# A streaming encoder trunk on one core: other chunks in one FFN, its last down products onto doubled x in PSUM, and eight weight sums made by an accumulating transfer

## The chip, the core and the metric

The kernel runs on one core of one Trainium2 chip. A core has a matrix engine (TensorE, in the profile PE, with its weight loads PEld), a vector engine (VectorE, DVE), an activation engine (ScalarE, ACT), GpSimd (POOL) and a queue that issues transfers (SyncE, SP); POOL and ACT issue some transfers too. SBUF is the core's working memory. PSUM is the memory into which PE's products go and in which they add up; here it holds eight banks of 128 x 512 f32, and DVE and ACT read it. The metric is the device time of one execution in microseconds (us); the time before is 2503.59 us, the median of 3 runs (2502.64 to 2503.89).

## The reference, cut to what matters

Two groups of streams (512 new frames, and 8 x 16 sample frames, together T = 640 columns) go through two layers; all is float32.

```
for l in range(2):
    x = x + 0.5 * swiglu1(rmsnorm(x))        # FFN "a{l}"
    x = x + mixer(rmsnorm(x))                # short convolution and chunk-band attention, gated
    x = x + 0.5 * swiglu2(rmsnorm(x))        # FFN "b{l}"
y = rmsnorm(x)

swiglu(h) = (silu(h @ w_g) * (h @ w_u)) @ w_down      # 1024 -> 2816 -> 1024
```

The outputs are y, the new keys and values, and the convolution's new state rows.

## The kernel before, in words

**Layout.** x is kept in SBUF as KT = 8 tiles of 128 x 640 (features by tokens); a product of one 128 x 128 weight block takes the tokens in two halves of HT = 320 columns. A float32 operand is split into a high part (hi, rounded by an ACT copy) and a low part (lo, what is left, by a DVE subtraction), and each product is three matmuls: hi by hi, lo by hi, hi by lo.

**The weight stream.** All weights are laid out on the host as one stream of 128 x 1024 rows (wst), in the order in which they are used. load (L253) lets SP fetch a row into a raw buffer; four buffers turn, so a row is fetched when DVE has read the one whose place it takes. prep (L308) makes the hi part (whi, ACT, L321) of the next slab, flush (L324) its lo part (wlo, DVE, L326); slab and begin call prep two slabs ahead of use. Both engines keep their own order: an instruction that waits holds up those behind it.

**Seven products for eight.** Where it can, the kernel multiplies 2 x 2 blocks with seven products instead of eight (block, L405, matmul L411; for the down weights down_rows, L966, matmul L982). For that the weights of a unit of two stream rows ra and rb are combined by source (L271) into four slabs: slab 0 is ra; slab 1 is a sum s = rb's two halves and ra's first (two adds); slab 2 is ra's first half plus rb's first half (L299, one DVE add of 128 x 512), and s plus ra's second half (L300); slab 3 is rb's second half. In such a unit gate_up (L773) makes one unit of 128 hidden features, gate and up together, in the order X11, X21, XN6, XT5, XT7, X22, XT4; after X11, XN6 and XT5 an ACT copy (c1, u2, c5: L850, L863, L866) takes a partial result from PSUM, and a later product adds to or overwrites that bank only after the copy. Hidden units that go into a down product by seven are made in pairs: Pair.product (L911) multiplies gate and up, and rounds the operand with an ACT copy (L926) and a DVE subtraction (L931); it runs in the tail of a unit, that is while the next unit is multiplied.

**Chunks.** The 22 hidden units of an FFN are taken in chunks (FFNS, L46). While the units of a chunk are made, the down products of the chunk before are put between them. A chunk of 4 that isn't the last goes down by seven products (by_seven, L81), in two calls of down_rows of 84 matmuls, which send part of their results to x by accumulating transfers of POOL (L1004) and add the rest with DVE (L1009). Any other chunk goes down by plain products (steps and product, L391 to L403, matmul L388): one per output tile m, with 6 matmuls for each hidden unit of the chunk, and then DVE's x[m] = x[m] + 0.5 * PSUM (L1119). The last chunk's are plain and come last, tile by tile, and the next stage's operands are made from each x[m] as soon as it is there (Expand.final, L539: square and gain on ACT, differences on DVE, hi parts on ACT, lo parts on DVE; Expand.weights, L594, prepares the next weights in the last tiles). PSUM has two accumulators of two banks for such products (acc) and four banks for the rest (att).

**Order.** PE's order is written out. DVE's and ACT's too (ORDERED, L213) at the beginning and the end of an FFN; between the third unit of its first by-seven chunk and the "cut" before its last products a scheduler orders them. POOL and SP are ordered by the scheduler.

**Where the diff touches.** FFNS (L46), source, prep and flush, multiply, steps and product (L384 to L403), Expand.weights (L594), gate_up (L773), Pair.product (L911), ffn (L1049). The FFNs named a0, b0, a1, b1 follow each other with a mixer between a and b of a layer. Line numbers in this section and in the profile before are those of the kernel before.

Of the kernel before, what the change touches and what calls it, by code (L numbers as in the profile page):

```python
# [44 lines left out]

FFNS = {"a0": ((4, 4, 4, 4, 4, 2), 4), "b0": ((2, 4, 4, 4, 8), 0),  # L46
        "a1": ((4, 4, 4, 4, 4, 2), 0), "b1": ((3, 4, 4, 4, 4, 3), 0)}
# [10 lines left out]

MARGIN = 2, 4

XT4, XN6, XT7, X21, X22, X11, XT5 = range(7)
# [128 lines left out]
def trunk(ctx: ExitStack, tc: tile.TileContext, xin, wst, small, pbias, samplebias, kcache, vcache,  # L190
# [59 lines left out]
    raws, ready = [], []  # L250
    sums, pool, spool = {}, [None], [None]

    def load(i):  # L253
# [17 lines left out]
    def source(i):  # L271
# [3 lines left out]
        if i not in sources:  # L275
# [6 lines left out]
            else:  # L282
# [14 lines left out]
                elif arg == 2:  # L297
                    if kind == "gu":
                        add(ra[:, h1], ra[:, h1], rb[:, h1])  # L299
                    add(ra[:, h2], sums.pop(n)[:, h1], ra[:, h2])  # L300
                    sources[i] = [(ra, whole)]
                else:
                    sources[i] = [(rb, h2)]
        return sources[i]

    pending = []

    def prep(i):  # L308
# [9 lines left out]
        for src, c in parts:  # L318
            d = slice(o, o + c.stop - c.start)
            o = d.stop  # L320
            ACT.copy(hi[:, d], src[:, c])  # L321
            pending.append((lo[:, d], src[:, c], hi[:, d]))

    def flush():  # L324
        for lo, src, hi in pending:
            DVE.tensor_tensor(out=lo, in0=src, in1=hi.bitcast(F32), op=ALU.subtract)  # L326
        pending.clear()

    used = [0]
# [53 lines left out]

    def multiply(ps, ws, xs, first, last):  # L384
        (wh, wl), (xh, xl) = ws, xs
        for j, (w, x) in enumerate(((wh, xh), (wh, xl), (wl, xh))):
            for a in range(2):
                PE.matmul(ps[:, a, :HT], w, x[:, a * HT : (a + 1) * HT],  # L388
                          start=first and j == 0, stop=last and j == 2)

    def steps(ps, ops, at=()):  # L391


        n = len(ops)
        for k, (xh, xl) in enumerate(ops):
            if k in at:
                at[k]()
            multiply(ps, tiles.take(), (xh, xl), k == 0, k == n - 1)
            yield

    def product(ps, ops, at=()):
        for _ in steps(ps, ops, at):
            pass  # L403
# [122 lines left out]
    class Expand(Stats):  # L526
# [67 lines left out]
        def weights(self, m):  # L594


            if m == KT - 3:
                source(used[0] + 3)
            elif m == KT - 1:
# [130 lines left out]
    def seven(n, bank, X, c1, u2, c5, first, second, third, last):  # L730
# [39 lines left out]
        with soon():  # L770
            last(pa)

    def gate_up(fp, n, ex, first, tails, put, j, pair, later, at):  # L773

# [72 lines left out]
        else:  # L847
# [14 lines left out]
            mul(pa, s1, 0, XN6, every, False, True)  # L862
            ACT.copy(u2, pa)  # L863
            spot("e3")
            mul(pc, s1, 1, XT5, every, True, True)
# [18 lines left out]
        def tail(weights=True):  # L884
# [5 lines left out]
            if pair:  # L890
                pair.product(n, u, g, hi, lo)
            else:
# [9 lines left out]
    class Pair:  # L902
# [7 lines left out]

        def product(self, n, u, g, hi, lo):  # L911
            if self.E is None:
# [12 lines left out]
            flush()  # L925
            ACT.copy(halves(hi), z[:, at])  # L926
            self.low(halves(lo), halves(hi), z[:, at])
            self.keep(kinds, hi, lo)

        def low(self, lo, hi, z):  # L930
# [118 lines left out]
    def ffn(name, fp, ex, goff, after, end=False):  # L1049
# [7 lines left out]
        hold[0] = True  # L1057

        mode = ExitStack()
        free = min(j for j in range(FT) if by_seven(name, j)) + 2  # L1060
# [8 lines left out]
        for what, a in ffn_order(name):  # L1069
# [6 lines left out]
            if what == "gu":  # L1076
                pair = None
                if by_seven(name, a):
                    i, odd = divmod(a - chunk_at(name, a)[0], 2)
                    if not odd:  # L1080
                        at = chunk_at(name, a)[0]
                        rows = at and by_seven(name, at - 1)
                        pairs[a] = Pair(fp, f"{name}_{a}", i, later, TURNS[i if rows else i + 2])
                    pair = pairs[a - odd]
                gate_up(fp, f"{name}_{a}", ex, a == plain, tails, act.__setitem__, a, pair, later,
                        a - chunk_at(name, a)[0])
# [12 lines left out]
            if end and js[0] == last:  # L1099
                nxt.all([act[j] for j in js])  # L1100
                break
            for m, js in a:
                if js[0] == last and m < 2 and first_two:
# [851 lines left out]
```

## Time and profile before

| what | value |
|---|---|
| three runs | 2502.64, 2503.59, 2503.89 us |
| the profiled execution | 2503.67 us |
| its span, first to last instruction | 2501.9 us |
| granted TensorE clock | 0.999 of full |
| HBM read, written | 222.70 MB, 7.94 MB |
| stretch of b0 | about 837 to 1255 us |
| stretch of a1 | about 1255 to 1667 us |

A row of the profile that describes a group of instructions has the line of the kernel, the engine, the operation, output <- inputs by the program's names (numbers left out, so paa is pa of an a FFN, pab of a b FFN, and lent or raw any of that name), the shape, the count, then the busy time, the mean duration of one in ns, and the idle time before them with what ended it. A row of the waits has who waited on whom: us in all, times, longest. In the timeline a row begins with the start and the duration. A row of the stretches has the stretch, its length, and for PE, PEld, DVE, ACT and POOL the busy time with the number of instructions, then the clock, the share of the transfer engines and GB/s. A row of the transfers has the issuing queue, the count, the size and the time from issue to landing. Matmuls overlap in the rows, so the distance between starts, not the duration, is what one costs. Windows of a row begin with the span at 0.

### The profile page before, as it was taken

To read this page: it belongs to the slowest core of one execution; us is meant where nothing else is said; L and a number is where in the kernel's file an instruction comes from. 1 tells how busy PE (TensorE), PEld (TensorE's weight loads), DVE (VectorE), ACT (ScalarE), POOL (GpSimd) and SP (SyncE) were. 2 spreads that over 40 slices of the span, in tenths; PEclk is the share of its full clock that TensorE was granted. 3 is DMA by queue.
4 is the path that set the end of the run, shared out by engine and by line. 5 is a ranking of instruction groups with operands and counts; after the bars stand their busy time and mean duration, and the time that the engine had idled before them with its cause. 6 is when DMAs were issued, how large, how long until landed. Compare 5 with 4: busy or idle time off the path is not lost.

```text
span 2501.9 us, 43874 instructions
## 1 busy us (share of the span) xinstructions
PE 2483.4 (99%) x17472; PEld 2433.1 (97%) x17472; DVE 2125.5 (85%) x3455; ACT 1321.4 (53%) x2065; POOL 240.0 (10%) x378
## 2 busy tenths in 40 slices
PE   9999999999999999999999999999999999999998
PEld 8999999889999999999999999998999999999998
DVE  7889998888777899998699999988887768899997
ACT  7445556665444545555455555566644455455553
POOL 0001112111000001100001111121110000011111
PEclk9999999999999999999999999999999999999999
DMA  4233445335222234443224343443342222244433
GB/s 146 76 102 102 123 117 127 108 109 169 77 91 92 72 100 116 111 106 101 85 77 109 110 122 101 116 119 117 121 156 85 77 93 79 87 112 110 121 101 103
DMA packets 101005, 265.47 MB, mean 106 GB/s; under 512 B 11360, under 2 KB 46816, under 8 KB 100800
## 3 DMA queue, kind: packets, MB, share of 16 engines
q1 hardware_dynamic: 69408, 220.76, 27.2%
q0 software_dynamic: 30528, 41.26, 8.9%
q8 instruction: 137, 2.24, 0.4%
q10 hardware_dynamic: 864, 0.65, 0.1%
q14 instruction: 68, 0.56, 0.1%
HBM read 222.70 MB, written 7.94 MB: 92 GB/s over the span
## 4 chain that ended last, share of the span: by engine, by line
PE 95%; DVE 2%; ACT 1%; issue 1%; DMA 1%; SPq 0%; DVEq 0%; ACTq 0%; POOLq 0%
PE pab L411 12%; PE paa L411 11%; PE pcb L411 6%; PE pca L411 6%; PE daa L982 5%; PE py L388 4%; PE po L388 4%; PE qa L411 4%; PE dab L982 4%; PE pdb L388 4%; PE pbb L411 3%; PE pba L411 3%; PE dca L982 3%; PE ma_cv L411 2%; PE pda L388 2%; PE pv L1425 2%
## 5 line engine op out<-in xcount | busy, mean ns | idle before, releaser
L321 ACT CAST whi<-raw 128x1024 fp32r<-128x1024 f32 (+1 forms) x566 | 509.6, 904 | 404.4 <-DVE raw L265 48.6
L326 DVE TENSOR_TENSOR wlo<-raw,whi 128x1024 fp32r<-128x1024 f32 (+1 forms) x566 | 585.8, 1038 | 147.2 <-ACT whi L321 142.2
L321 ACT CAST whi<-s 128x1024 fp32r<-128x1024 f32 (+1 forms) x152 | 144.3, 950 | 267.3 <-issue 89.5
L411 PE MATMUL pab<-xhib,whi 128*128 128x320 f32 x704 | 218.0, 310 | 0.0
L411 PE MATMUL pab<-xlob,whi 128*128 128x320 f32 x704 | 217.4, 309 | 0.0
L411 PE MATMUL pab<-xhib,wlo 128*128 128x320 f32 x704 | 217.4, 309 | 0.0
L411 PE MATMUL paa<-xhia,whi 128*128 128x320 f32 x640 | 198.1, 310 | 0.8 <-ACT c_a L863 0.5
L411 PE MATMUL paa<-xloa,whi 128*128 128x320 f32 x640 | 197.6, 309 | 0.0
L411 PE MATMUL paa<-xhia,wlo 128*128 128x320 f32 x640 | 197.6, 309 | 0.0
L326 DVE TENSOR_TENSOR wlo<-s,whi 128x1024 fp32r<-128x1024 f32 (+1 forms) x152 | 166.3, 1094 | 2.8 <-ACT whi L321 2.8
L1004 POOL DMA_DIRECT2D x<-c_b x56 | 49.2, 1016 | 1070.0 <-DVE x L1009 786.4
L1004 POOL DMA_DIRECT2D x<-c_a x72 | 63.4, 1013 | 832.2 <-ACT whi L321 508.7
L411 PEld LDWEIGHTS pab<-xhib,whi 128*128 128x128 f32 x704 | 132.2, 188 | 1.3 <-issue 0.9
L411 PEld LDWEIGHTS pab<-xlob,whi 128*128 128x128 f32 x704 | 132.2, 188 | 0.0
L411 PEld LDWEIGHTS pab<-xhib,wlo 128*128 128x128 f32 x704 | 132.2, 188 | 0.0
L411 PEld LDWEIGHTS paa<-xhia,whi 128*128 128x128 f32 x640 | 120.1, 188 | 1.8 <-ACT c_a L863 0.7
L411 PEld LDWEIGHTS paa<-xloa,whi 128*128 128x128 f32 x640 | 120.2, 188 | 0.0
L411 PEld LDWEIGHTS paa<-xhia,wlo 128*128 128x128 f32 x640 | 120.1, 188 | 0.0
L411 PE MATMUL pcb<-xhib,wlo 128*128 128x320 f32 x352 | 108.9, 309 | 0.0
L411 PE MATMUL pcb<-xlob,whi 128*128 128x320 f32 x352 | 108.7, 309 | 0.0
L411 PE MATMUL pcb<-xhib,whi 128*128 128x320 f32 x352 | 108.7, 309 | 0.0
L265 DVE TENSOR_TENSOR raw<-raw,raw 128x512 f32<-128x512 f32 x152 | 103.8, 683 | 2.6 <-DMA raw<-in_wst 2.3
(680 smaller groups left out, 7949.8 us busy)
## 6 DMA issues: line engine op xcount, KB each, us to landing
raw<-in_wst SPq DMA_DIRECT2D x378, 512.0 KB, 3.6
x<-c_a POOLq DMA_DIRECT2D x72, 160.0 KB, 4.5
x<-c_b POOLq DMA_DIRECT2D x56, 160.0 KB, 4.1
kc<-in_kcache SPq DMA_DIRECT2D x32, 256.0 KB, 4.8
vc<-in_vcache SPq DMA_DIRECT2D x16, 512.0 KB, 4.6
x<-u_a POOLq DMA_DIRECT2D x36, 160.0 KB, 4.1
x<-u_b POOLq DMA_DIRECT2D x28, 160.0 KB, 4.2
bias<-in_pbias POOLq DMA_DIRECT2D x16, 256.0 KB, 3.8
```

What stands on the lines that cost most here:

```text
L265: DVE.tensor_tensor(out=out, in0=a, in1=b, op=ALU.add)
L321: ACT.copy(hi[:, d], src[:, c])
L326: DVE.tensor_tensor(out=lo, in0=src, in1=hi.bitcast(F32), op=ALU.subtract)
L388: PE.matmul(ps[:, a, :HT], w, x[:, a * HT : (a + 1) * HT], start=first and j == 0, stop=last and j == 2)
L411: PE.matmul(ps, a, b, start=start and kp == 0 and j == 0, stop=stop and kp == NP - 1 and j == 2, skip_group_check=True)
L982: PE.matmul(ps[u], w, y, start=start and i == 0 and j == 0, stop=i == 1 and j == 2, skip_group_check=True)
L1004: POOL.dma_start(x[ms[2 * u + r]][:, cols], z[:, u], accum_op=ALU.add)
L1425: PE.matmul(pv[t], xx[:, t * P : (t + 1) * P], w[:, kk * AW : (kk + 1) * AW], start=c == 0 and kk == 0 and j == 0, stop=c == KT // 2 - 1 a ...
```

## The change

- FFN b0 takes its 22 units in chunks of 4, 4, 4, 4, 6 instead of 2, 4, 4, 4, 8. A chunk of 6 is last, so its down products are plain; the four chunks of 4 go by seven.
- The last products of an FFN whose last chunk is over 4 and that is followed by another FFN (b0 alone): ACT writes 2 * x[m] into the accumulator first (seed), the products add to it, and ACT takes x[m] = 0.5 * PSUM. The last tile is made as before. Two seeds stand ahead of the last gate/up unit, the others one tile ahead.
- For gate/up units 1 to 4 of b0 and a1 (counted from 0) the sum of ra's and rb's first halves is made by POOL: it loads the one from memory into a buffer (lent, one buffer) and loads the other onto it with an accumulating transfer. It is issued when slab 2 of the unit before is prepared. slab 2's hi and lo parts are then made in two halves.
- In the first unit of an FFN that has a pair, the rounding of that pair's operand (ACT copy and DVE subtraction) is held back from the tail until u2 of the next unit is copied.
- Expand.weights looks up the slab that it sums ahead (the next slab 1) instead of counting three ahead.

```diff
-FFNS = {"a0": ((4, 4, 4, 4, 4, 2), 4), "b0": ((2, 4, 4, 4, 8), 0),
+FFNS = {"a0": ((4, 4, 4, 4, 4, 2), 4), "b0": ((4, 4, 4, 4, 6), 0),
         "a1": ((4, 4, 4, 4, 4, 2), 0), "b1": ((3, 4, 4, 4, 4, 3), 0)}
+LEAN = {"b0": 5, "a1": 5}
...
+    lent, lean, at = {}, set(), 0
+    for name, (_, units) in zip([f"{k}{l}" for l in range(L) for k in "amb"], stages()):
+        ns = []
+        for z in units:
+            if z == "gu":
+                ns.append(at)
+            at += 2 if z in ("gu", "mix") else 1
+        if name in LEAN:
+            lean.update(ns[1 : LEAN[name]])
+
+    def lend(n):
+        z = lent[n] = pool[0].tile([P, CH // 2], F32, tag="lent", name=f"lent{n}", bufs=1)
+        POOL.dma_start(z, wst[n][:, h1])
+        POOL.dma_start(z, wst[n + 1][:, h1], accum_op=ALU.add)
...
                 elif arg == 2:
-                    if kind == "gu":
+                    if kind == "gu" and n not in lean:
                         add(ra[:, h1], ra[:, h1], rb[:, h1])
                     add(ra[:, h2], sums.pop(n)[:, h1], ra[:, h2])
-                    sources[i] = [(ra, whole)]
+                    sources[i] = [(lent.pop(n), h1), (ra, h2)] if n in lean else [(ra, whole)]
...
     def prep(i):
...
+        if slabs[i][2] == 2 and slabs[i][0] == "gu" and i + 2 < len(slabs) and slabs[i + 2][1] in lean:
+            lending.append(slabs[i + 2][1])
     def flush():
...
+        for n in lending:
+            lend(n)
+        lending.clear()
...
+    def seed(ps, m, scale):
+        ACT.activation(two(ps), halves(x[m]), AF.Copy, scale=scale)
-    def multiply(ps, ws, xs, first, last):
+    def multiply(ps, ws, xs, first, last, seeded=False):
...
-                          start=first and j == 0, stop=last and j == 2)
+                          start=first and j == 0 and not seeded, stop=last and j == 2,
+                          skip_group_check=seeded)
...
             if m == KT - 3:
-                source(used[0] + 3)
+                source(next(i for i in range(used[0], len(slabs)) if slabs[i][0] == "gu" and slabs[i][2] == 1))
...
+    held = []
     def gate_up(fp, n, ex, first, tails, put, j, pair, later, at):
...
             mul(pa, s1, 0, XN6, every, False, True)
             ACT.copy(u2, pa)
+            for t in held:
+                t()
+            held.clear()
             spot("e3")
...
-                pair.product(n, u, g, hi, lo)
+                pair.product(n, u, g, hi, lo, held if first else None)
...
-        def product(self, n, u, g, hi, lo):
+        def product(self, n, u, g, hi, lo, held=None):
...
-            ACT.copy(halves(hi), z[:, at])
-            self.low(halves(lo), halves(hi), z[:, at])
+            def parts():
+                ACT.copy(halves(hi), z[:, at])
+                self.low(halves(lo), halves(hi), z[:, at])
             self.keep(kinds, hi, lo)
+            if held is None:
+                parts()
+            else:
+                held.append(parts)
...
+        def begun(name, j, m):
+            pds[m] = acc(f"pd{name}_{j}_{m}")
+            seed(pds[m], m, 2.0)
+
+        def seeded_down(name, a, js, nxt):
+            for m, _ in a:
+                if m + 1 < KT - 1 and m:
+                    begun(name, js[0], m + 1)
+                end = m == KT - 1
+                pd = acc(f"pd{name}_{js[0]}_{m}") if end else pds.pop(m)
+                product(pd, [act[j] for j in js], seeded=not end)
+                nxt.weights(m)
+                if end:
+                    DVE.scalar_tensor_tensor(out=halves(x[m]), in0=two(pd), scalar=0.5,
+                                             in1=halves(x[m]), op0=ALU.mult, op1=ALU.add)
+                else:
+                    ACT.activation(halves(x[m]), two(pd), AF.Copy, scale=0.5)
+                    flush()
+                nxt.final(m)
...
+                if after is not None and a == FT - 1 and chunks[-1] > 4:
+                    for m in range(2):
+                        begun(name, last, m)
...
+            if nxt and len(js) > 4:
+                seeded_down(name, a, js, nxt)
+                continue
```

More of the change, by code (lines that the diff above doesn't have):

```diff
@@ L304, in source @@
         return sources[i]
-    pending = []
+    pending, lending = [], []
     def prep(i):
@@ L388, in multiply, with steps @@
                 PE.matmul(ps[:, a, :HT], w, x[:, a * HT : (a + 1) * HT],
-                          start=first and j == 0, stop=last and j == 2)
-    def steps(ps, ops, at=()):
+                          start=first and j == 0 and not seeded, stop=last and j == 2,
+                          skip_group_check=seeded)
+    def steps(ps, ops, at=(), seeded=False):
         n = len(ops)
@@ L397, in steps, with product @@
                 at[k]()
-            multiply(ps, tiles.take(), (xh, xl), k == 0, k == n - 1)
+            multiply(ps, tiles.take(), (xh, xl), k == 0, k == n - 1, seeded)
             yield
-    def product(ps, ops, at=()):
-        for _ in steps(ps, ops, at):
+    def product(ps, ops, at=(), seeded=False):
+        for _ in steps(ps, ops, at, seeded):
             pass
@@ L1057, in ffn @@
         hold[0] = True
+        pds = {}
+        def begun(name, j, m):
[16 more added lines that the diff above has]
+                nxt.final(m)
         mode = ExitStack()
```

## The prediction

> **What bounds the kernel now.** I read the page first, then PE's waits, then the chain of waits, then the busy time by stretches of the second FFN of layer 0 (tiles named b0) and the first FFN of layer 1 (a1), which are what the diff touches.
>
> ```profile
> span 2501.9 us, 43874 instructions
> PE 2483.4 (99%) x17472; PEld 2433.1 (97%) x17472; DVE 2125.5 (85%) x3455; ACT 1321.4 (53%) x2065; POOL 240.0 (10%) x378
> PE 95%; DVE 2%; ACT 1%; issue 1%; DMA 1%; SPq 0%; DVEq 0%; ACTq 0%; POOLq 0%
> 1198.42 56.32 PE pdb L388 x384
> PE dab L982 <- DVE x L1009: 0.2, 1, 0.2
> PE paa L411 <- ACT c_a L863: 0.5, 1, 0.5
> PE pca L411 <- ACT c_a L866: 0.4, 2, 0.2
> PE paa L411 <- ACT c_a L850: 0.3, 1, 0.3
> 842.00:1255.00 413.00, 412.81 (x2845) 411.34 (x2844) 358.94 (x545) 210.14 (x299) 31.79 (x36) 1.00 0.37 102
> 1255.00:1290.00 35.00, 34.22 (x264) 32.70 (x263) 31.14 (x48) 21.13 (x33) 0.00 (x0) 1.00 0.26 81
> 1290.00:1320.00 30.00, 29.81 (x204) 29.55 (x203) 29.39 (x48) 16.02 (x25) 0.00 (x0) 1.00 0.27 83
> 1380.00:1660.00 280.00, 280.00 (x1910) 279.75 (x1909) 255.93 (x403) 150.00 (x214) 44.89 (x52) 1.00 0.45 115
> ```
>
> TensorE (PE) is the bound: 99% busy and 95% of the chain. So a change gains only by taking matmuls away or by ending one of PE's few waits, and it loses by making a new one. The row of the stretch holds, after its length, PE, PEld, DVE, ACT and POOL busy time: in b0 PE lacks 0.2 us in all, in the opening of a1 (1255 to 1320) it lacks 1.0 us, and there DVE is at 29.39 of 30 us. Later in a1 DVE stands at 91% (255.93 of 280) and PE waits for nothing. The chain's piece prices a matmul: 56.32 us / 384 = 146.7 ns (the rows' 310 ns overlap).
>
> **The change, part by part.**
>
> *Chunks.* Chunks of 2 and 8 units were handled with plain products: (2 + 8) x 8 output tiles = 80 tile products of 6 matmuls, 480. Now only the 6 are plain: 48 x 6 = 288. A fourth chunk of 4 goes by the seven-product scheme: two calls of down_rows, each 7 x 12 = 84 matmuls, 168. 480 - 288 - 168 = 24 matmuls fewer; the built instruction order agrees (16891 to 16867 on PE). 24 x 146.7 ns = **-3.5 us**. The gate/up part keeps its count. Helper work grows (pair operands, weight sums) and b0 comes to look like a1, where the steady stretch hides it.
>
> *Held pair split and the order on ACT.* What a wait costs is more than its idle time:
>
> ```profile
> 1275.55 0.31 PE L411 MATMUL pca<-xhia,wlo 128*128 128x320 f32 x1
> 1276.32 0.41 PE L411 MATMUL paa<-xhia,whi 128*128 128x320 f32 x1 [0.46 <-ACT c_a L863]
> 1285.08 0.31 PE L411 MATMUL pba<-xhia,wlo 128*128 128x320 f32 x1
> 1285.70 0.41 PE L411 MATMUL paa<-xhia,whi 128*128 128x320 f32 x1 [0.32 <-ACT c_a L850]
> 1285.95 0.30 PE L411 MATMUL paa<-xloa,whi 128*128 128x320 f32 x1
> ```
>
> From 1285.08 to 1285.95 are 0.87 us where two pitches are 0.29: 0.58 lost beside 0.32 shown, so 0.26 is to be added to each wait. The four waits of a1 (0.5 + 0.4 + 0.3 = 1.2 shown) cost 1.2 + 4 x 0.26 = 2.2 us. All four wait for an ACT copy that stood behind another ACT instruction. At 1275 the copy of u2 stood behind the pair's operand copy (ahia), which waited for DVE; the held closure puts that copy behind u2. In the two waits at L866 the c5 copy stood behind whi and then ahia; in the new order ahia precedes whi, which waits for PE anyway. The fourth (L850) is the subject of the next part. I count **-2.2 us** for the old waits and price anew what stands at the fourth. The wait on dab in b0 (0.2 shown, 0.46 with the addition) hangs on a landing of x<-c_b and need not come back: **-0.2**, half of it.
>
> *The weight sum by a transfer.* For eight units (gate/up units 1 to 4 of b0 and a1) a DVE add of 128x512 goes. In its place POOL issues two transfers of 256 KB to one buffer, the second accumulating, each waiting for what precedes it: the first for DVE to be done with the buffer's last content, the second for the first to land. ACT's copy of the half waits for the second. Behind that copy, on ACT, stand the other half's copy, the Silu and the c1 copy that releases PE. POOL has nothing else then: in the built order only one pair stands ahead of another unit's x transfers (the first of a1, ahead of b0's), and those are not due. The first pair in each FFN is issued long ahead. The tight one is unit 2's. In a1:
>
> ```profile
> 1275.10 1.82 DVE L326 TENSOR_TENSOR wlo<-raw,whi 128x1024 fp32r<-128x1024 f32 x2
> 1271.77 0.69 DVE L265 TENSOR_TENSOR raw<-raw,raw 128x512 f32<-128x512 f32 x1
> 1272.37 0.69 DVE L265 TENSOR_TENSOR raw<-s,raw 128x512 f32<-128x512 f32 x1
> 1283.65 1.05 ACT L321 CAST whi<-raw 128x1024 fp32r<-128x1024 f32 x1 [0.55 <-PE paa L411]
> 1284.61 0.73 ACT L880 ACTIVATE ga<-ga 128x640 f32<-128x640 f32 x1
> 1285.24 0.40 ACT L850 COPY c_a<-paa 128x320 f32<-128x320 f32 x1
> 1285.55 0.62 ACT L321 CAST whi<-raw 128x512 fp32r<-128x512 f32 x1
> 1276.34 0.33 SPq L261 DMA_DIRECT2D raw<-in_wst  x1
> 1276.95 0.33 SPq L261 DMA_DIRECT2D raw<-in_wst  x1
> ```
>
> Release: the add at 1271.77 took 0.60 to the next row; without it the splits start at 1274.5, and the lent half, which comes first, is read by 1274.5 + 0.69 = 1275.2. Need: the matmul at 1285.70 without its own loss (0.58) and that at 1276.32 (0.72) is due at 1284.4. Ahead of it stand two half copies (some 0.52 each, 0.62 less the overlap), the Silu (0.63 to the next row) and the c1 copy (0.40), 2.1 us: the sum must have landed by **1282.3**, 7.1 us after the release. DVE and ACT reach these places just in time otherwise (the add of this unit goes too), so the old wait at L850 ends unless the transfer makes one.
>
> How long do two such transfers take? No accumulating load from memory is in the trace. The nearest are a plain POOL load of 256 KB and accumulating transfers of 160 KB:
>
> ```profile
> bias<-in_pbias POOLq DMA_DIRECT2D x1, 256.0 KB, 2.9
> 956.89 1.79 POOL L1004 DMA_DIRECT2D x<-c_b  x2 [343.75 <-DVE x L1009]
> x<-c_b POOLq DMA_DIRECT2D x1, 160.0 KB, 5.8
> raw<-in_wst SPq DMA_DIRECT2D x1, 512.0 KB, 4.4
> x<-c_b POOLq DMA_DIRECT2D x1, 160.0 KB, 2.8
> 1337.26 1.75 POOL L1004 DMA_DIRECT2D x<-c_a  x2 [198.78 <-ACT whi L321]
> x<-c_a POOLq DMA_DIRECT2D x1, 160.0 KB, 3.0
> ```
>
> Alone, one takes 2.8 to 3.0 us. But the transfer of 956.89 took 5.8: a weight load of SP's (the 4.4 row) was issued 0.46 us behind it, and the POOL transfer landed only about 0.9 us after that load. The one of 1337.26, with a load 1.2 us behind it, was not held up (3.0). In the new order SP's two loads (now at 1276.34 and 1276.95, each at the end of a DVE split) follow the release by 0.6 and 1.2 us. 0.6 is nearer to 0.46, so I take the first transfer as held up: the loads land 3.7 and 4.4 us after issue, at 1279.5 and 1280.8, so it lands between 1280.4 and 1281.7; the second, with no load beside it, 3.0 to 3.4 us later, at 1283.4 to 1285.1. That is 1.1 to 2.8 us late: **+2.0 us**, and the same in b0, whose opening has the same order: **+4.0 us**. Ends: 0 (neither held up) and some 4.5 each (both held up). Units 3 and 4 have 9 us and more, since their release comes earlier in the unit, and the loads follow it by 1.3 us.
>
> [...]
>
> *Doubled x in PSUM.* In b0's last products the DVE evacuation goes, and ACT gets a seed and an evacuation instead.
>
> ```profile
> 1198.00:1255.00 57.00, 57.00 (x390) 57.00 (x390) 39.23 (x53) 27.98 (x35) 0.00 (x0) 1.00 0.20 66
> L1119 DVE SCALAR_TENSOR_TENSOR x<-pdb,x 128x640 f32<-128x640 f32 x8 | 6.6, 824 | 13.2 <-PE pdb L388 13.1
> L321 ACT CAST whi<-raw 128x1024 fp32r<-128x1024 f32 x8 | 8.4, 1046 | 2.9 <-PE pdb L388 2.2 <-PE pab L411 0.7
> L610 ACT ACTIVATE sqa<-x 128x640 f32<-128x640 f32 x6 | 4.4, 741 | 15.7 <-DVE x L1119 15.7
> L559 ACT ACTIVATE xoa<-x,sm 128x640 f32<-128x640 f32 x3 | 2.5, 820 | 0.0
> L567 ACT CAST xhia<-xoa 128x640 fp32r<-128x640 f32 x3 | 2.2, 728 | 0.1
> L576 ACT CAST xhia<-xoa 128x960 fp32r<-128x960 f32 x3 | 3.0, 997 | 2.9 <-DVE xoa L571 2.9
> ```
>
> A product takes 36 x 146.7 ns = 5.28 us instead of 7.04, eight take 42.2. ACT had 28.0 us there; two weight copies go (2.1), seven evacuations and five seeds come (the other two stand before the last gate/up unit), at about 0.75 from the 640-element rows: 9.0. So 35 of 42 us. DVE loses seven evacuations (5.8). No ACT write to PSUM is in the trace; 0.5 to 0.85 bounds it. The seed of product m + 2 uses the bank that product m leaves, and PE needs it 5.28 us later. Behind an even m: evacuation, square, gain, copy, seed, 3.7 us with a short wait: in time. Behind an odd m also the 960-element copy, which waited 1.0 us for DVE: 0.75 + 0.74 + 0.82 + 0.73 + 1.0 + 0.75 = 4.8, plus some 0.5 of that wait and signals: about 5.3. So it just misses at m = 1 and 3: **+0.5 us**, between 0 and 1.5.
>
> Sum: -3.5 - 2.2 - 0.2 + 4.0 + 0.5 = **-1.4 us**. The profiled execution took 2503.67 us (span 2501.9 and 1.8 around it), 0.08 over the median 2503.59 of the three runs. 2503.6 - 1.4 = **2502.2 us**.
>
> **Rivals.**
> - *The sum is in time.* Loads and POOL transfers share the engines, the pair takes 6 to 7 us. [...] Against: the rows at a lag near 0.5. Then -3.5 - 2.2 - 0.2 + 0.5 = -5.4: 2498.2; with no seed wait 2497.7.
> - *Every sum is late (slower).* Both transfers of a pair take the held-up price, 5.8 us, in each unit: 11.8 with signals. Unit 2 is 4.7 late, unit 4, with about 9.3, 2.5; two FFNs: 14.4. It decides once a pair takes over 10 us. -3.5 - 2.2 - 0.2 + 14.4 + 0.5 = +9: 2512.6. For it: an accumulating load must read both sides, and no row shows one. Against: no load is issued near the second transfer.
> - *ACT bounds the last products.* With a seed at the upper price and a weight copy ahead of an evacuation in each step, a step takes 6.2 us instead of 5.28; six steps, +5.5 in place of 0.5: 2507.2. Against: 35 of 42 us.
> - *The count does not fall* can't be: it is in the built program.
>
> **How the numbers follow.** Likeliest 0.54, own range 2499 to 2505; in time 0.26; every sum late 0.12; ACT-bound 0.08. A measurement of this kernel can tell about 0.2% (5.0 us) from no change. In the second case three quarters lie beyond that: faster 0.20. Within: 0.54 + 0.06 + 0.08 = 0.68. Slower 0.12. The range 2497.2 to 2507.5 takes in all but the late sums and the edges.
>
> **What would show it.** PE's count 24 lower per trace order; PE's waits at L863 and L866 in a1's opening gone; the copy of lent in unit 2 of b0 and a1 waiting for its DMA, with PE waiting 1 to 3 us for the c1 copy behind it; first transfers landing 5 to 6.5 us after issue, second ones near 3; waits of PE for the seed below 0.5 each. Wrong if PE waits for lent in no unit (time near 2498), or in units 3 and 4 too (over 2508), or if b0's steady units show PE waits that a1's do not.

## The result, and the profile after

The changed kernel takes 2507.80 us (median of 20 runs, 2506.18 to 2510.68), the kernel before 2503.82 us (20 runs, 2502.64 to 2504.91). The ratio is 1.0016, 95% interval 1.0010 to 1.0022: 4.0 us slower. 2502.2 us was predicted, 1.4 us faster, with a range from 2497.2 to 2507.5; the change went the other way and ended just above the range.

The page of the changed kernel, and its waits of TensorE (who waited on whom: us in all, times, longest). Lines have moved: L878, L891 and L897 are the copies c1, u2 and c5 (L850, L863 and L866 before), L413 and L437 the plain and the seven-product matmuls.

```profile
span 2507.3 us, 43956 instructions
PE 2483.9 (99%) x17448; PEld 2433.3 (97%) x17448; DVE 2128.8 (85%) x3478; ACT 1341.0 (53%) x2101; POOL 262.3 (10%) x406
```

```profile
PE pab L437 <- ACT c_b L878: 2.8, 1, 2.8
PE paa L437 <- ACT c_a L878: 1.8, 1, 1.8
PE paa L437 <- DVE xloa L617: 0.8, 1, 0.8
PE pdb L413 <- DVE alob L230: 0.6, 1, 0.6
PE pca L437 <- DVE wlo L344: 0.3, 1, 0.3
PE dab L1020 <- DVE x L1047: 0.2, 1, 0.2
```

There are 24 matmuls fewer, and the old waits for u2 and c5 are gone from a1. In their place stand a wait of 2.8 us in b0 and one of 1.8 us in a1, both for c1 of unit 2, and three small ones at the end of b0 and the beginning of a1. The timeline of the long one, in b0:

```profile
857.15 0.68 DVE L344 TENSOR_TENSOR wlo<-lent,whi 128x512 fp32r<-128x512 f32 x1
858.25 0.55 POOL L266 DMA_DIRECT2D lent<-in_wst  x1 [222.69 <-DVE wlo L344]
863.83 0.90 POOL L267 DMA_DIRECT2D lent<-in_wst  x1 [5.02 <-DMA lent<-in_wst]
868.01 0.62 ACT L337 CAST whi<-lent 128x512 fp32r<-128x512 f32 x1 [3.00 <-DMA lent<-in_wst]
869.05 0.73 ACT L911 ACTIVATE gb<-gb 128x640 f32<-128x640 f32 x1
869.69 0.40 ACT L878 COPY c_b<-pab 128x320 f32<-128x320 f32 x1
870.14 0.42 PE L437 MATMUL pab<-xhib,whi 128*128 128x320 f32 x1 [2.84 <-ACT c_b L878]
871.43 0.46 PE L437 MATMUL pab<-xhib,wlo 128*128 128x320 f32 x1
871.69 0.47 PE L437 MATMUL pab<-xhib,whi 128*128 128x320 f32 x1
```

This is the chain that the prediction named: DVE leaves lent, POOL issues the load, waits for its landing, issues the accumulating one; ACT's copy of the sum waits 3.0 us for it, and behind that copy stand the Silu and the c1 copy for which TensorE waits. The last two rows show what the prediction did not have: 1.3 us after TensorE has resumed, matmuls start 260 ns apart instead of 147 (below this is called half pitch). In the stretches behind the wait (stretch, its length, PE busy with instructions, granted clock, share of the transfer engines, GB/s) the granted clock falls to 0.50 and comes back:

```profile
868.00:870.00 2.00, 0.00 (x0) 1.00 0.00 0
870.00:872.00 2.00, 1.85 (x11) 0.85 0.43 119
872.00:874.00 2.00, 2.00 (x9) 0.50 0.78 217
874.00:876.00 2.00, 2.00 (x13) 0.79 0.81 228
```

13 matmuls at half pitch lose 1.5 us; the same happens in a1 at 1291.12, 13 matmuls and 1.6 us. The transfers of unit 2 (issue to landing), in b0 with the weight load issued 0.21 us behind the first, then in a1:

```profile
lent<-in_wst POOLq DMA_DIRECT2D x1, 256.0 KB, 5.2
raw<-in_wst SPq DMA_DIRECT2D x1, 512.0 KB, 4.8
...
lent<-in_wst POOLq DMA_DIRECT2D x1, 256.0 KB, 4.1
...
lent<-in_wst POOLq DMA_DIRECT2D x1, 256.0 KB, 4.3
...
lent<-in_wst POOLq DMA_DIRECT2D x1, 256.0 KB, 3.9
```

Where the time went by stretches, from the start of the first matmul of one FFN to that of the next (b0: first pab to first paa; a1: first paa to first pda):

| kernel | b0, us | a1, us |
|---|---|---|
| before | 836.80 to 1254.58: 417.78 | to 1653.09: 398.51 |
| changed | 837.24 to 1257.74: 420.50 | to 1659.34: 401.60 |
| difference | +2.72 | +3.09 |

Together +5.8 us of the span's +5.4; all that lies outside differs by -0.4. The profiled execution (2509.03 us) is 1.2 us over its median.

### The profile page after: what moved, and what is told of

It is laid out like the page before. It is cut to its first block, busy times and chain, and to the rows that moved or that the text cites. A ratio compares the mean times of both kernels' runs of the same rounds, so it can differ in the third digit from the quotient of the medians.

```text
span 2507.3 us, 43956 instructions
## 1 busy us (share of the span) xinstructions
PE 2483.9 (99%) x17448; PEld 2433.3 (97%) x17448; DVE 2128.8 (85%) x3478; ACT 1341.0 (53%) x2101; POOL 262.3 (10%) x406
## 5 line engine op out<-in xcount | busy, mean ns | idle before, releaser
L437 PE MATMUL pab<-xhib,whi 128*128 128x320 f32 x704 | 218.1, 310 | 2.8 <-ACT c_b L878 2.8
L437 PE MATMUL pab<-xhib,wlo 128*128 128x320 f32 x704 | 217.6, 309 | 0.0
L437 PE MATMUL pab<-xlob,whi 128*128 128x320 f32 x704 | 217.6, 309 | 0.0
L437 PE MATMUL paa<-xhia,whi 128*128 128x320 f32 x640 | 198.6, 310 | 1.8 <-ACT c_a L878 1.8
L437 PE MATMUL paa<-xloa,whi 128*128 128x320 f32 x640 | 198.4, 310 | 0.8 <-DVE xloa L617 0.8
L437 PE MATMUL paa<-xhia,wlo 128*128 128x320 f32 x640 | 198.3, 310 | 0.0
L1042 POOL DMA_DIRECT2D x<-c_b x64 | 56.2, 1014 | 811.8 <-DVE x L1047 471.3
L437 PEld LDWEIGHTS pab<-xhib,whi 128*128 128x128 f32 x704 | 132.2, 188 | 4.2 <-ACT c_b L878 3.1
L437 PEld LDWEIGHTS pab<-xlob,whi 128*128 128x128 f32 x704 | 132.3, 188 | 0.0
L437 PEld LDWEIGHTS pab<-xhib,wlo 128*128 128x128 f32 x704 | 132.3, 188 | 0.0
L437 PEld LDWEIGHTS paa<-xhia,whi 128*128 128x128 f32 x640 | 120.6, 188 | 2.5 <-ACT c_a L878 2.1
L437 PEld LDWEIGHTS paa<-xloa,whi 128*128 128x128 f32 x640 | 120.7, 189 | 1.0 <-DVE xloa L617 1.0
L437 PEld LDWEIGHTS paa<-xhia,wlo 128*128 128x128 f32 x640 | 120.7, 189 | 0.0
L437 PE MATMUL pcb<-xhib,wlo 128*128 128x320 f32 x352 | 109.3, 310 | 0.0
L437 PE MATMUL pcb<-xhib,whi 128*128 128x320 f32 x352 | 109.2, 310 | 0.0
L437 PE MATMUL pcb<-xlob,whi 128*128 128x320 f32 x352 | 109.1, 310 | 0.0
L281 DVE TENSOR_TENSOR raw<-s,raw 128x512 f32<-128x512 f32 x154 | 104.9, 681 | 0.0
```

The source lines that it names most:

```text
L281: DVE.tensor_tensor(out=out, in0=a, in1=b, op=ALU.add)
L437: PE.matmul(ps, a, b, start=start and kp == 0 and j == 0, stop=stop and kp == NP - 1 and j == 2, skip_group_check=True)
L1042: POOL.dma_start(x[ms[2 * u + r]][:, cols], z[:, u], accum_op=ALU.add)
```

## The experiments

**Theory A**: the pair of transfers of unit 2 is late, TensorE waits for it, and the wait itself puts TensorE to half pitch for some 3.4 us; together 3.0 + 1.5 in b0 and 2.0 + 1.6 in a1, 8.1 us. The rivals: the order on ACT and DVE is what is late; the transfers cost by their traffic; the half pitch has another cause. The medians, each compared with the kernel before on the same chip:

| kernel | us | ratio to before, 95% | b0 | a1 |
|---|---|---|---|---|
| no transfers (e1_no_lean) | 2504.97 | 1.0004 (0.9995 to 1.0013) | 417.56 | 399.79 |
| transfers for units 2 to 4 (e2_lean_from_2) | 2501.50 | 0.9993 (0.9984 to 1.0002) | 416.36 | 398.32 |
| no doubled x (e3_no_seed) | 2507.79 | 1.0016 (1.0008 to 1.0025) | 422.11 | 400.08 |
| second transfer plain (e4_plain_second) | 2503.38 | 0.9997 (0.9988 to 1.0006) | 416.99 | 399.53 |
| chunks alone (e5_chunks_only) | 2504.05 | 1.0000 (0.9991 to 1.0009) | 417.19 | 399.89 |
| transfers for units 1, 3, 4 (e6_lean_1_3_4) | 2501.82 | 0.9992 (0.9983 to 1.0001) | 416.35 | 398.58 |
| two orders, everywhere (e8_reordered) | 2499.98 | 0.9986 (0.9977 to 0.9995) | 416.13 | 396.85 |
| units 2 to 4, no doubled x (e9_from_2_no_seed) | 2501.28 | 0.9989 (0.9980 to 0.9998) | 416.00 | 398.29 |
| units 2 to 4, not held (e10_from_2_not_held) | 2502.70 | 0.9995 (0.9987 to 1.0004) | 416.78 | 398.67 |
| 1, 3, 4, no doubled x, two orders (e11_best) | 2501.25 | 0.9990 (0.9981 to 0.9999) | 415.63 | 398.28 |
| units 2 to 4, two orders in a1 (e13_two_orders) | 2500.57 | 0.9987 (0.9978 to 0.9996) | 416.17 | 396.79 |

### The late pair taken away

```diff
-            lean.update(ns[1 : LEAN[name]])
+            lean.update(ns[2 : LEAN[name]])
```

> The changed kernel with the transfers for units 2, 3 and 4 only: unit 1's sum is DVE's again, so unit 2's pair is the first into the buffer and waits for nothing. Theory A: lent for unit 2 lands long before its copy, no wait of TensorE in unit 2, no slow stretch: 2507.8 less 8.1 is 2499.7; up to 2501 if the add in unit 1 brings a wait of 0.5 us in each FFN. Rival 1 (the transfers cost by their traffic, wherever they are issued): 2506 to 2508. Rival 2 (the half pitch has another cause than the wait): the waits go, the two stretches at 290 ns stay, 2502.9.

Measured 2501.50 us, 6.3 less than the changed kernel. Unit 2's pair is now the first into the buffer and is issued long before; ACT's copies follow each other. TensorE's waits from 830 to 1660 us are the last four of the changed kernel's list and two new ones:

```profile
PE pab L437 <- DVE wlo L344: 0.2, 1, 0.2
PE paa L437 <- DVE wlo L344: 0.2, 1, 0.2
```

Both long waits are gone, and both stretches of half pitch with them; unit 1's add brings these two of 0.2 us (0.38 lost each). Three of the four pairs of each FFN still move, so the traffic as such does not explain the loss, and the half pitch went with the waits, so it needs no other cause here. The gain is 7.4 us in the traced b0 and a1 (4.14 + 3.28), 6.3 in the medians; the median is 0.5 above the end that was expected for waits of 0.5 us in unit 1. The 8.1 us came from a traced execution that was itself 1.2 over its median, which is enough to account for that.

### No transfers at all

```diff
-LEAN = {"b0": 5, "a1": 5}
+LEAN = {}
```

> The changed kernel with the eight weight sums made by DVE again (no transfers into lent); chunks, held rounding and doubled x stay. Theory A (the late pair of transfers in unit 2 of b0 and a1 costs its wait, 3.0 and 2.0 us, and behind each wait TensorE runs 13 matmuls at half pitch, 1.5 and 1.6 us): both waits and both slow stretches go, minus 8.1 us from 2507.8; the wait for the c1 copy that the kernel before has there (0.45 us) may come back in each, so 2499.7 to 2500.7. Theory B (the sums are not what costs; the order on ACT and DVE after the last products makes the copies late anyway): the waits for the c1 copy stay over 1.5 us and the time is 2505 to 2508.

Measured 2504.97 us: neither theory. The long waits are gone as A says, but 4 to 5 us that A had not counted come back. The waits of TensorE in b0, without that on dab (a1 shows the same four of wlo and c5):

```profile
PE pab L437 <- DVE wlo L344: 0.6, 2, 0.3
PE pdb L413 <- DVE alob L230: 0.6, 1, 0.6
PE pcb L437 <- ACT c_b L897: 0.4, 2, 0.2
```

With the sums on DVE, wlo of units 1 and 3 and the c5 copies of units 3 and 5 are late again, 1.6 us in each FFN by the matmuls' starts, some 2 with the pitch behind each. So the transfers are worth more than the prediction knew: 3.5 us between this kernel and that with units 2 to 4. And the waits for c5, which the prediction gave to the new order on ACT, stay in this kernel, which has that order; it is DVE's relief that removes them.

### What makes the pair slow

```diff
-        POOL.dma_start(z, wst[n + 1][:, h1], accum_op=ALU.add)
+        POOL.dma_start(z, wst[n + 1][:, h1])
```

> The changed kernel with the second transfer of each pair as a plain load in place of the accumulating one, so that lent holds the second row's half and not the sum: it leaves that addition out. Theory A (a pair is slow because of the weight loads beside it and because two landings follow each other; adding costs little): second transfers still 3.9 and 4.1 us in unit 2 (above 3.5), the waits within 0.5 us of 2.8 and 1.8, 2506.5 to 2508. Rival (adding reads the buffer too and costs about 1 us a transfer, 3.9 to 4.1 against 2.9 for a plain one alone): second transfers near 3.0, waits 1.8 and 0.8, the slow stretch in a1 gone: 2503.5 to 2505.

Measured 2503.38 us; the rival is nearer. TensorE's two waits, then the first and second transfer of unit 2 in b0 and in a1:

```profile
PE paa L437 <- ACT c_a L878: 1.3, 1, 1.3
PE pab L437 <- ACT c_b L878: 0.9, 1, 0.9
```

```profile
lent<-in_wst POOLq DMA_DIRECT2D x1, 256.0 KB, 4.1
...
lent<-in_wst POOLq DMA_DIRECT2D x1, 256.0 KB, 3.2
...
lent<-in_wst POOLq DMA_DIRECT2D x1, 256.0 KB, 4.3
...
lent<-in_wst POOLq DMA_DIRECT2D x1, 256.0 KB, 3.4
```

Plain, the second takes 3.2 and 3.4 us against 4.1 and 3.9. Over all eight pairs the second transfers take 4.84 us on average in the changed kernel (3.94 to 5.97) and 4.04 here (3.19 to 5.23): adding costs 0.8, of which 0.33 is POOL's longer issue (0.87 us instead of 0.54, which the time to landing includes). The firsts stay at 4.1 and 4.3 in unit 2, where a weight load follows within 0.35 us, and take 2.9 to 3.3 in units 3 and 4, where it follows after 0.78 us or more. So a load close behind goes with a longer transfer, here too; that the load is the cause is a comparison of places, for no run moved the load alone. With waits of 0.95 and 1.28 us no stretch of half pitch follows, which is why 0.7 us a pair (and a first transfer of 4.1 for 5.2 in b0) moves the median by 4.4.

### The half pitch measured by itself

The kernel before, with the same c1 copy made k times more in single units, so that TensorE waits there; 20 units in one kernel, 24 in the other. Neither has a transfer into lent. Each was executed once, with the trace (2587.85 and 2584.50 us).

```diff
-            ACT.copy(c1, pa)
+            for _ in range(1 + DOSE.get(n, 0)):
+                ACT.copy(c1, pa)
```

> The kernel before, in which 20 single units of a0, b0, a1 and b1 make their c1 copy 4 to 14 times more (the same copy again, about 0.40 us each), so that TensorE waits there for about 0.40 k - 1.2 us: 0.4 (k = 4) to 4.4 us (k = 14). Theory A (an idle stretch halves TensorE's pitch for 3 to 5 us afterwards when it fills about half or more of a window of some 3.4 us that runs by itself): no slow stretch behind waits up to 1.3 us, one behind some of those of 1.6 to 2 us, one behind all of 2.8 us and more, each with 13 to 20 matmuls at 265 ns and 1.5 to 2.4 us lost, independent of the wait's length. [...] Rival (the slow stretch comes from the transfers): none at all.

> The kernel before with 24 units in which the c1 copy is made 5 to 8 times more, for waits of TensorE of about 1.4 (4 units), 1.9 (8), 2.35 (8) and 2.8 us (4). Theory A (an idle stretch halves the pitch if at least some half of a window of 3.4 us that runs by itself falls into it, so the share grows with the wait): none of 4, 1 to 4 of 8, 3 to 7 of 8, 4 of 4. Rival (a fixed length decides): none below some length between 1.4 and 2.8 us, all above it.

Two waits of the same length from the first of these kernels, the first at 1012.16 in b0, the second at 1504.86 in a1; then the stretches behind each:

```profile
1012.16 0.42 PE L414 MATMUL pab<-xhib,whi 128*128 128x320 f32 x1 [1.89 <-ACT c_b L854]
...
1504.86 0.41 PE L414 MATMUL paa<-xhia,whi 128*128 128x320 f32 x1 [1.90 <-ACT c_a L854]
```

```profile
1012.00:1014.00 2.00, 1.84 (x12) 1.00 0.53 176
1014.00:1016.00 2.00, 2.00 (x16) 1.00 0.86 334
1504.80:1506.80 2.00, 1.94 (x11) 0.80 0.50 164
1506.80:1508.80 2.00, 2.00 (x9) 0.50 0.32 129
```

The same wait is followed by half pitch once and not the other time. All waits of both kernels (a pitch is the distance between two starts; lost is the sum of what the pitches behind the wait, after the first, have over 147 ns):

```
wait, us        waits   followed by half pitch   lost there, us
0.98 to 1.44      7        0                      -
1.88 to 1.90     11        7                      1.5 to 1.6
2.34 to 2.36     12        6                      1.2 to 1.6
2.61 to 2.81      5        4                      1.2 to 1.6
3.31 to 5.56      9        9                      1.3 to 2.6
```

So transfers are not needed for half pitch, 26 of the 37 waits from 1.88 us up were followed by it, and no fixed length of the wait decides; nor does the share grow steadily between 1.9 and 2.4 us, as A had it for the second kernel (six of its seven waits of 1.9 us were slowed, where A had 1 to 4 of 8, and one of 2.61 was not). What decides shows in the times at which the slow stretches end: in each kernel they differ by multiples of 3.413 us, to within 0.13 (12 ends in the first, 14 in the second). The changed kernel's trace has the same length: there the clock is granted at 0.50 from 871.41 to 874.83 and from 1291.25 to 1294.67, 3.413 us each, with the two starts 419.84 us apart, 123 times that. Let a window be one step of this grid. Then one rule fits all 44 waits: after a window at full clock that held 1.88 us or more of the idle time the next ran at half pitch, after one that held 1.85 or less it did not. A wait that straddled a boundary was split and could stay below. Behind a window that itself ran at half pitch less was enough: with 0.7 us (the wait that ends at 2411.16 in the first kernel) and 1.4 us (1385.64 in the second) left over in it, a second one followed at 0.50, which makes the longest losses; with 0.4 us or less it did not. The changed kernel agrees: of the wait in b0 (867.30 to 870.14) 2.1 us lie in the window that ends at 871.41, where the clock falls, and at 871.43 the half pitch begins. In a1 1.8 us lay in one window and were enough, so the bound in these runs is about 1.8, within the 0.13 by which the grid is known. In the trace of the next section's first kernel (no doubled x) the same wait of a1, 1.85 us, lies across a boundary with 1.6 us on one side, and no half pitch follows.

### Doubled x in PSUM

```diff
-                if after is not None and a == FT - 1 and chunks[-1] > 4:
+                if False:
...
-            if nxt and len(js) > 4:
+            if False:
```

> The changed kernel with the last products of b0 as before: plain products and DVE's evacuation, no doubled x in PSUM; the rest stays. Theory A (ACT is short in the last products: two waits of 0.25 us at odd tiles, and the last operands come late into a1, 0.9 and 0.4 us lost there): 1.9 us less than 2507.8, so 2505.9, with no wait for xloa near the beginning of a1. Rival (those waits come from steps of 5.3 us instead of 7.0, whoever evacuates, and DVE would be late in ACT's place): 2507.5 to 2509.5.

> The kernel with transfers for units 2 to 4 (2501.5 us), with the last products of b0 as before, DVE evacuating. Theory A (doubled x costs two waits of 0.25 us and nothing else; DVE has room for seven evacuations in 43 us): 0.5 to 0.8 less, 2500.7 to 2501.1, waits for xloa and wlo at a1's beginning the same. Rival (it takes work off DVE that is late at a1's beginning): 2501.5 to 2503.

From the changed kernel's row, PE's weight loads wait for the seed twice:

```profile
PEld pdb L413 <- ACT pdb L407: 0.7, 2, 0.4
```

On top of the changed kernel the median stays (2507.79, runs from 2504.89 to 2510.51), as the rival had it: the run in the trace has 20 matmuls at half pitch and a second late pair (unit 4, 1.0 us) in b0 and no half pitch in a1, which buries the part. On top of units 2 to 4, where nothing is late, the last products (first pdb to first paa) take 43.11 us instead of 43.83: doubled x costs 0.72 us in the trace (the two waits for the seed), 0.2 in the medians, between the two forecasts and within the scatter of the runs. In both kernels the waits for xloa (0.8) and wlo (0.3) at a1's beginning are the same with and without it, so these were not ACT's, as A had it.

### The chunks alone, and the order on DVE

```diff
-"b0": ((2, 4, 4, 4, 8), 0)
+"b0": ((4, 4, 4, 4, 6), 0)
```

> The kernel before with the chunks of b0 alone changed to 4, 4, 4, 4, 6 (and the slab that is summed ahead looked up). Theory A (the 24 matmuls fewer are given back where the steps are shorter and where b0's opening now looks like a1's): -3.5, +0.7 (the last unit's low part comes late for the first last product), +1.4 (xloa and the weights late at the beginning of a1), +2.0 (waits in b0's units 1 to 5 like those of a1): +0.6, 2504.0 to 2505.3. Rival (the count decides): -3.5 + 0.5, 2500.4 to 2501.5.

Measured 2504.05 us against 2503.97: the 24 matmuls bring nothing by themselves. b0's waits in this kernel, with the lines of the kernel before:

```profile
PE pdb L388 <- DVE alob L229: 0.5, 1, 0.5
PE pab L411 <- ACT c_b L863: 0.5, 1, 0.5
PE pcb L411 <- ACT c_b L866: 0.4, 2, 0.2
PE pab L411 <- ACT c_b L850: 0.3, 1, 0.3
```

The last three rows are a1's old waits but for the tiles' names: b0 with chunks of 4 at its beginning has a1's opening. The first row and a1's 1.38 us more (399.89 against 398.51) come with the shorter steps. How, the order on DVE at the end of b0 shows, in the changed kernel:

```profile
1257.26 0.82 DVE L617 TENSOR_TENSOR xloa<-xea,xhia 128x640 fp32r<-128x640 f32 x1
1257.99 0.68 DVE L281 TENSOR_TENSOR raw<-raw,raw 128x512 f32<-128x512 f32 x1
1258.60 0.68 DVE L281 TENSOR_TENSOR raw<-s,raw 128x512 f32<-128x512 f32 x1
1259.20 0.81 DVE L1113 SCALAR_TENSOR_TENSOR x<-pdb,x 128x640 f32<-128x640 f32 x1
```

TensorE leaves the last product at 1257.74, and its evacuation stands behind two sums for the next weights until 1259.20. With steps of 7.0 us these sums were done in time; in the kernel before the evacuation starts 0.20 us behind the last product, which ends at 1254.58:

```profile
1252.91 0.69 DVE L265 TENSOR_TENSOR raw<-s,raw 128x512 f32<-128x512 f32 x1
1254.78 0.82 DVE L1119 SCALAR_TENSOR_TENSOR x<-pdb,x 128x640 f32<-128x640 f32 x1
```

Two orders were changed: the sums for slab 2 one output tile earlier, and the low part of the last unit's operand ahead of that of the weights.

```diff
+            elif m == KT - 2 and self.name == "a1":
+                source(next(i for i in range(used[0], len(slabs)) if slabs[i][0] == "gu" and slabs[i][2] == 2))
...
-                flush()
+                if j < FT - 1:
+                    flush()
                 split(hi, lo, u)
+                flush()
```

> The kernel with transfers for units 2 to 4 (2501.5 us), in which two things on DVE change their order: the last unit of an FFN makes the low part of its operand before that of the weights, and the sum for slab 2 of the next FFN is made one output tile earlier, ahead of the last evacuation. Theory A (the waits of 0.6 us for alob and of 0.8 and 0.3 us for xloa and wlo at the end of b0 come from DVE's order, too late for steps of 5.3 us): they go, less 0.7 and 1.4: 2499.4 to 2500.2. Rival (DVE or ACT is simply full there): the waits stay under other names, 2501 to 2502.5.

> Transfers for units 2 to 4, doubled x kept, and the two orders on DVE (last unit's low part first; slab 2's sum of a1 one tile earlier) with the second of them in a1 alone, so that in b0 and b1 the sums stand as in the changed kernel (the run with both orders everywhere added into a row of b0 and b1 before it had been split, which changed the output). Theory A (the waits for xloa and wlo at a1's beginning, 0.9 and 0.4 us, come from the two adds that stand on DVE ahead of the last evacuation): gone again, 2501.5 - 1.5 = 2500.0, 2499.6 to 2500.6. Rival (what went there went because the sums of b0 and b1 moved as well): the waits stay, 2501.0 to 2501.8.

The first of these runs had no condition on a1, so that in b0 and b1 a sum went into a row before its low part was made, which changes the values; 2499.98 us. With the condition, 2500.57 us, ratio 0.9987 (0.9978 to 0.9996), the fastest kernel here that computes the reference's outputs, 3.3 us under the kernel before and 7.2 under the changed one. DVE around the same place:

```profile
1248.72 0.69 DVE L281 TENSOR_TENSOR raw<-s,raw 128x512 f32<-128x512 f32 x1
1249.32 1.22 DVE L344 TENSOR_TENSOR wlo<-s,whi 128x1024 fp32r<-128x1024 f32 x1
...
1252.32 0.82 DVE L617 TENSOR_TENSOR xloa<-xea,xhia 128x640 fp32r<-128x640 f32 x1
1253.06 0.82 DVE L1117 SCALAR_TENSOR_TENSOR x<-pdb,x 128x640 f32<-128x640 f32 x1
```

The sums go into a place where DVE had time, the evacuation follows the product (which ends at 1252.79) after 0.27 us instead of 1.46, no wait for xloa is left, and a1 is 1.53 us shorter than with units 2 to 4 (396.79 against 398.32): the order was the cause. The other order does half of what was expected of it: the wait for alob falls from 0.6 to 0.3 us.

### Three more

> The changed kernel with transfers for units 1, 3 and 4 and unit 2's sum by DVE: the one pair that has too little time is not issued. Theory A (without any transfer unit 2 showed no wait, unit 1 one of 0.38 us; so unit 2's sum is the one that DVE can make for nothing): no wait in units 1 to 5 of b0 and a1, 1.0 us less than with units 2 to 4, 2500.3 to 2500.9. Rival (what DVE does for unit 2 moves the wait): one of 0.3 to 0.5 us in unit 2, 2501.2 to 2501.8.

With units 1, 3 and 4 (the set in place of the range in lean.update) 2501.82 us: the rival. A wait for c1 of unit 2 comes in each FFN (0.3 us shown, 0.47 lost by the starts), the one that a1 had before, in place of unit 1's 0.38.

> The kernel with transfers for units 2 to 4 (2501.5 us), with the rounding of the first pair's operand in the tail again, as in the kernel before, not held back. Theory A (held back, it takes 0.63 us of wait at the u2 copy in unit 1 of b0 and a1 away, of which the wait for wlo there, 0.38, is left): the wait at the u2 copy returns, 0.25 to 0.6 more in each FFN, 2502.0 to 2502.8. Rival (with less on DVE the order on ACT does not matter): 2501.3 to 2501.7.

With None in place of "held if first else None" 2502.70 us: the wait for the u2 copy is back (0.5 us shown in b0 and in a1), b0 0.42 and a1 0.35 us longer, as A says. The held rounding is worth about 0.8 us.

> Transfers for units 1, 3 and 4; no doubled x in PSUM; the last unit's low part ahead of that of the weights; the sum for slab 2 of a1 one tile earlier, in a1 alone. Theory A (each of these takes away a wait of its own): 2501.5 - 1.0 (unit 1) - 0.7 (two waits of 0.25 at the seeds and their edges) - 1.5 (as with those two orders before) = 2498.3, 2497.8 to 2499.2. Rival (they share one limit, DVE, which now also evacuates): 2499.5 to 2501.

2501.25 us: nearer to the rival, 0.25 beyond its end. Without doubled x TensorE reaches a1 earlier, and DVE, which now evacuates all eight tiles, is nearly as late as before (xloa, 0.6 us for 0.8). That speaks for doubled x relieving DVE there, but this kernel also differs from the last in the units whose sums are transferred.

## Why the prediction was wrong, step by step

| term, us | predicted | found |
|---|---|---|
| 24 matmuls fewer | -3.5 | -3.5 |
| old waits of a1 | -2.2 | -2.2 |
| wait on dab in b0 | -0.2 | 0 |
| late pair of unit 2 in b0 and a1 | +4.0 | 3.1 + 2.1 = +5.2 |
| half pitch behind these waits | not counted | 1.5 + 1.6 = +3.2 |
| doubled x | +0.5 | +0.7 |
| shorter steps: alob in b0, xloa and wlo in a1 | not counted | 0.8 + 1.4 = +2.2 |
| sum | -1.4 | +5.6 |

What was found is read from the counts and starts in the traces. The stretches b0 and a1 say +5.8; the medians say +4.0, since -0.4 lies outside and the traced execution was 1.2 over its median.

- **The late pair** was right in mechanism and place, with 1.1 to 2.8 us of lateness forecast in each FFN and 3.0 and 2.0 found (3.15 and 2.12 us between two starts, less 0.15; 0.1 more in the next pitch). The second transfer was mis-sized: 3.0 to 3.4 forecast "with no load beside it", 4.1 and 3.9 measured. Adding costs 0.8 on average, and no row of before held such a transfer; the end of 4.5 in each FFN covered it. The first transfers, forecast as held up (5.2 to 6.5 us), took 5.2 and 4.3. So the pair came out inside its forecast in sum (9.7 and 8.7 us from the first issue to the second landing, 8.2 to 9.9 forecast), in part by luck: a first too dear in a1 and seconds too cheap in both.
- **"What a wait costs"** is the step that failed most. The prediction took idle time plus 0.26 us, from waits of at most 0.46 us shown. Waits that put about 1.8 us or more into one window of 3.413 us also paid 1.2 to 2.6 us of half pitch, 26 of them in the two kernels with repeated copies. The prediction's own 1.1 to 2.8 us of lateness crossed that bound, and 3.2 us on top of -1.4 alone turn the sign.
- **"The steady stretch hides it"**, said of b0 coming to look like a1, failed in the opening: chunks alone give b0 a1's waits, and the gain of 3.5 is gone (2504.05). In the changed kernel the transfers cover that, as the kernel without them shows.
- **The product of 5.28 us** was used to price ACT's seeds (0.5 forecast, 0.7 found) and not asked what else had relied on 7.04 us: the last unit's low part and the next FFN's sums on DVE. That is 2.2 us.
- **The old waits** went as forecast in sum, but not for the reason given: the held rounding removes the one at u2, the transfers those at c5.
- **The rivals.** "The sum is in time" gave 2498.2: with the late pair out of the way it is 2501.5, and 2500.6 with the two orders as well. "Every sum is late" is not what happened; units 3 and 4 show no wait in the changed kernel's row. But their pairs were hardly quicker than unit 2's: their second transfers, for which loads had been issued 0.6 to 2.6 us ahead, took 5.1 to 6.0 us, and the pairs 8.5 to 9.5 us from the first issue to the second landing, so it was their slack that saved them, and in the trace of the kernel without doubled x that of unit 4 in b0 was used up. "ACT bounds the last products", at 2507.2, is nearest in time and wrong in cause.
- The signs named in advance held for the count, the waits at u2 and c5, the copy of lent and the seeds; not for the second transfers ("near 3"), and for the first ones ("5 to 6.5 us") in b0 alone.

## What to carry to other kernels

On an engine that is 99% busy, price a new wait by more than its length: ask whether it can put some 1.8 us of idle time into one stretch of 3.413 us, the window found here, and if so add what that cost here, 1.5 us in b0 and 1.6 in a1. A transfer that replaces an add pays only where its buffer is free early enough; here, of four such sums in a row, the one with the least time between its buffer's release and its use decided, and dropping its neighbour (unit 1's) gave back 6.3 us. When a step gets shorter, look at everything that was fitted into the old one, on every engine.

## What the runs showed of the hardware

- **The clock of TensorE** fell to 0.50 (265 ns from start to start for 147) for a window of 3.413 us after a window at full clock with about 1.8 us or more of idle time; in two cases a second window at 0.50 followed. Within each of the two kernels with repeated copies the slow stretches end on one grid of 3.413 us (to within 0.13), wherever the waits lie, so the same wait of 1.9 us cost 1.5 us more in 7 of 11 cases. No wait up to 1.44 us was followed by half pitch; 26 of 37 from 1.88 us up were, 18 of these shorter than 3.413 us.
- **Accumulating from memory** by a POOL transfer took 4.84 us on average for 256 KB against 4.04 plain in the same places, and POOL needed 0.87 us to issue it instead of 0.54:

```profile
L267 POOL DMA_DIRECT2D lent<-in_wst x8: 847/867/899, 634.7 to 1309.8; - x8
```

```profile
L267 POOL DMA_DIRECT2D lent<-in_wst x8: 536/538/554, 634.3 to 1304.2; - x8
```

The first row is the changed kernel, the second that with a plain second transfer (duration in ns: least, median, most).
- **A load beside a transfer** (no run moved the load alone): in b0's unit 2 the first transfer landed 5.15 us after its issue, with a weight load issued 0.21 us behind it that landed at 5.0 by the same clock; in units 3 and 4, with the load 0.76 us or more behind, it took 2.9 to 3.5 us. Unit 1's, issued long before they are needed, do not fit as cleanly: 4.0 us with the load 0.74 behind and 3.8 with it 0.34 behind. The two transfers of unit 2 together took 9.2 us in b0 and 8.2 in a1.
